# Expert weights as one 8 KB piece per partition, with features, scale, shift and router in that order

## The chip, the cores and the metric

The kernel runs on one core of a Trainium2 chip. Its time is the device time of one execution in microseconds (us), as the median of several runs; lower is better. A core has a matrix engine (PE, with its weight loads listed apart as PEld), a vector engine (DVE), a scalar engine (ACT), GpSimd (POOL), SyncE (SP), which here issues nearly all transfers, and 16 DMA engines that carry them from the chip's main memory (HBM) into the on-chip memory SBUF, which has 128 partitions.

## What is computed

A transformer block with a mixture of experts is followed by a second block of two layers, all in float32, on 256 tokens of 1024 features. The part that the change is about, cut from the reference:

```python
h = modulate(x, norm_ffn_pre, shift, scale)      # rms_norm(x, g) * (1 + scale) + shift
logits = jnp.dot(h, w_router) + b_router
top_logit, top_idx = lax.top_k(logits, TOP_K)    # 4 of 32 experts for each token
gates = jax.nn.softmax(top_logit, axis=-1)
# for each expert e, on the tokens that chose it:
g = h_e @ w_gate[e] + b_gate[e]                  # w_gate, w_up, w_down: 1024 x 1024 each
u = h_e @ w_up[e] + b_up[e]
a = (min(g, 7) * sigmoid(1.702 * min(g, 7))) * (clip(u, -7, 7) + 1)
y_e = a @ w_down[e] + b_down[e]                  # summed over a token's four experts by its gates
```

`shift` and `scale` are two of six modulation vectors, `silu(c) @ w_mod + b_mod`, of 1024 values each. The weights of the 32 experts are 403 MB, all of which are read once.

## The kernel before

**The stream of weights.** Weights pass through a ring of 21 tiles of 128 x 2048 floats (1 MB), in five pools. The class `Stream` has a list of jobs in the order in which the matmuls use them. `pump` (L164) issues the next job's DMA on SP's queue as soon as the job's pool has a free tile; `get` hands the oldest chunk to the matmuls, and `free` gives its tile back. What an engine computes has the order in which the code is written: there is no scheduler. Transfers run as far ahead as free tiles let them.

**The first stage** (`pre_project`, `pre_attend`, `pre_finish`) computes the modulation vectors, the projections, the attention, and the router. Modulation weights come in 24 chunks: eight early ones of 8 x 256 columns per partition, and sixteen late ones, one row of 2048 columns per partition (`add_late`). The late ones are summed on PE (`mod_mm`, L321) or, for the other half, on DVE (`msum`, L314). `mod_fin` then copies the sum to `mrow` (L331), turns it on PE with four transposes into one PSUM bank (L334), and adds the bias `b_mod` on DVE (L338). `mod` then holds a column for each 128 features: column k has features 128 k to 128 k + 127. `gains` (L794 to L796) makes `a2`, (1 + scale) times the gain `norm_ffn_pre`, in the same columns. `pre_finish` turns the tokens' features x into columns (`turned`, L902) and multiplies them with the router's weights `wr` (L913), which are loaded feature 128 k + p into partition p; `router` (L858) multiplies the shift with them.

**The expert stage** (`experts`). Each expert takes twelve chunks of 1 MB: four of `w_gate`, four of `w_up`, four of `w_down`. A chunk is 256 rows of the weight matrix; partition p takes rows p and 128 + p of it (`expert_chunks`), two pieces of 4 KB. An expert works on up to 64 tokens at a time; expert 16 in the order, the one with the most tokens, is run twice on the same chunks, so there are 33 passes. `gather_k` (L1292) gathers the columns of two experts' tokens with one-hot matmuls, where x is the stationary operand (the weight load) and the one-hot matrix `pm` moves, and ACT applies `a2` and the shift on the way out. `up_mm` (L1209) multiplies a chunk of gate or up weights, which moves, with the gathered columns; `turn_h` (L1243) transposes the hidden values, with h as the stationary operand; `down_mm` (L1220) multiplies the down weights; a one-hot matmul (L1362) adds the result into its tokens' rows. Small work (gathers, transposes, scatters) is popped from a list between the chunks. Within a chunk, matmul j takes row pair member j, which must be the feature of column 2 q + j of the gathered tokens: that is what ties the order of rows in a chunk to the order of features everywhere else.

**The last stage** is the second block (`even`, `mlp`, `odd`), whose weights follow the experts' in the same stream.

Of the kernel before, what the change touches and what calls it, by code (L numbers as in the profile page):

```python
# [19 lines left out]
P = 128  # L20
# [97 lines left out]
def one(v, src):  # L118
    return [(v, src)]
# [99 lines left out]
        self.pump()  # L219


class Kernel:
    def __init__(self, tc, I, dbg=None):
        self.tc, self.nc, self.I, self.dbg = tc, tc.nc, I, dbg or {}
# [103 lines left out]
    def mod_fin(self, acc, n):  # L328
        nc = self.nc
        mrow = self.mrow  # L330
        nc.scalar.copy(mrow, acc)  # L331
        b = self.bank()
        for j in range(4):
            nc.tensor.transpose(b[:, j * P : (j + 1) * P], mrow[:, j * P : (j + 1) * P], self.c("ident"))  # L334
        v = b.rearrange("p (j g i) -> p j g i", j=4, g=4)
        o = self.mod[:, 0, 16 * n : 16 * n + 16].rearrange("p (g j) -> p j g", g=4)
        bb = self.V("b_mod")[:, 16 * n : 16 * n + 16].rearrange("p (g j) -> p j g", g=4)
        nc.vector.tensor_tensor(o, v[:, :, :, 0], bb, OP.add)  # L338

    def split_rows(self, hi, lo, v):  # L340

# [23 lines left out]
    def pre_project(self, A, B):  # L365
# [8 lines left out]
        for nm, n in rows:  # L374
            src = I[nm]
            if len(src.shape) == 2:
# [16 lines left out]
        tp = lambda a: a.rearrange("(t p) d -> p t d", p=P)  # L393
        nc.sync.dma_start(out=x, in_=tp(I["x"][0]))
        nc.sync.dma_start(out=xc, in_=tp(I["ctx"][0]))
        also = {("i", 3): [(pc, I["pre"]), (self.wf, I["w_fourier"][0].rearrange("(i g) c d -> (g c) i d", g=2))],
                ("q", 2): [(self.wr, kp(I["w_router"][0])), (self.br, I["b_router"])], ("k", SMALL): self.post_small(),
                ("o", 3): self.expert_bias_in(B)}

        def add(nm, q, cols, f, split=None):  # L400
# [227 lines left out]
    def pre_attend(self, B, C):  # L628
# [95 lines left out]
            self.modulation(MODS[6 + t])  # L724
        st.free(2)
        self.post_turn()
        for i in range(2):
            mix[i] = B.tile([P, 2048], F32R, tag=f"lk{i}", name="mix").rearrange("p (k t) -> p k t", k=KD)
        nc.scalar.activation(C.tile([P, 3], F32, tag="mx", name="mx", bufs=4)[:, 0:1], self.eps[1e-6], AF.Exp)
# [63 lines left out]
        def gains():  # L793
            nc.vector.tensor_tensor(gc, mod[:, 0, 16:24], self.V("norm_attn_post"), OP.mult)  # L794
            nc.vector.tensor_tensor(self.g2, mod[:, 0, 40:48], self.V("norm_ffn_post"), OP.mult)
            nc.vector.scalar_tensor_tensor(self.a2, mod[:, 0, 32:40], 1.0, self.V("norm_ffn_pre"), OP.add, OP.mult)  # L796

        fills = {u: [self.modulation] * FILLS[u] + [gains] * (u == 4) for u in range(5)}
        due = []
# [47 lines left out]
    def pre_finish(self, B, C, R):  # L847
# [50 lines left out]
        def turned(t):  # L898
            for h in range(2):
                b = self.bank()  # L900
                for k in range(4):
                    nc.tensor.transpose(b[:, k * P : (k + 1) * P], x[:, t, (4 * h + k) * P : (4 * h + k + 1) * P], ident)  # L902
                nc.scalar.copy(xT[:, 4 * h : 4 * h + 4, t * P : (t + 1) * P], b.rearrange("p (k t) -> p k t", k=4))

        def norm(t):
# [260 lines left out]
    def expert_chunks(self):  # L1166

        I, st, nc = self.I, self.stream, self.nc
        self.reg = {}

        def src(nm, p, q):
            def f(v):
                w = I[nm][0]
                if p < FIXED:
                    return one(v, w[p, q * 256 : (q + 1) * 256].rearrange("(k p) f -> p k f", p=P))
                if p not in self.reg:
                    self.reg[p] = nc.values_load(self.ids[0:1, p : p + 1], engines=(ENG.SP,), min_val=0, max_val=E - 1)
                return one(v, w[bass.ds(self.reg[p], 1), q * 256 : (q + 1) * 256].rearrange("o (k p) f -> p (o k) f", p=P))
            return f

        for p in range(E + 1):
            if p < E:
                for nm in ("w_gate", "w_up"):
                    for q in range(4):
                        st.add((2, 1024), src(nm, p, q))
            if p:
                for q in range(4):
                    st.add((2, 1024), src("w_down", p - 1, q))
# [50 lines left out]
    def turn_h(self, M, h):  # L1239
        nc = self.nc  # L1240
        b = self.bank("tr", "x")
        for j in range(4):
            nc.tensor.transpose(b[:, j * P : (j + 1) * P], h[:, j * P : (j + 1) * P], self.c("ident"))  # L1243
        ht = M.tile([P, 4, P], F32, tag="ht", name="ht", bufs=2)
        nc.scalar.copy(ht.rearrange("p a b -> p (a b)"), b)
        return ht
# [39 lines left out]
    def gather_k(self, xg, pm, k, n, m):  # L1286

        nc = self.nc
        b = self.bank("xg", "r" if m == 2 else "x")
        for j in range(m):  # L1290
            for t in range(2):
                nc.tensor.matmul(b[:, n * j : n * j + n], self.x[:, t, (k + j) * P : (k + j + 1) * P], pm[:, t, 0:n], start=(t == 0), stop=(t == 1))  # L1292
        for j in range(m):
            nc.scalar.activation(xg[:, k + j], b[:, n * j : n * j + n], AF.Identity,  # L1294
                                 bias=self.mod[:, 0, 24 + k + j : 25 + k + j], scale=self.a2[:, k + j : k + j + 1])
# [163 lines left out]
    def overflow(self, M):  # L1459
# [3 lines left out]
        with tc.If(self.more > 0):  # L1463
# [3 lines left out]
            with tc.For_i(0, self.more, 1) as j:  # L1467
                e = nc.values_load(self.ids[0:1, bass.ds(j + (E + 1), 1)], engines=(ENG.Activation,), min_val=0, max_val=E - 1)

                def weights(nm, q):  # L1470
                    w = self.yw
                    nc.scalar.dma_start(out=w, in_=I[nm][0][bass.ds(e, 1), q * 256 : (q + 1) * 256].rearrange("o (k p) f -> p (o k) f", p=P))
                    return w

                sc = M.tile([E + 1, 2], F32, name="scol")
# [1031 lines left out]
```

## Time and profile before

| | us |
|---|---|
| median of 3 runs | 1805.74 |
| lowest, highest | 1804.57, 1810.54 |
| profiled execution, its own time | 1805.48 |
| its span, from the first to the last instruction | 1803.70 |

| engine | busy us | share of the span |
|---|---|---|
| PE matmuls | 1721.6 | 95% |
| PE weight loads | 1031.0 | 57% |
| DVE | 744.8 | 41% |
| ACT | 583.3 | 32% |
| POOL | 22.8 | 1% |

The core read 550.71 MB from HBM in the span, 306 GB/s in the mean. Shares over the whole span mix three stages with different limits, so they are read stage by stage: the rate of the transfers in each window, and in the chain of waits (followed back from the last instruction) whether a stage's steps are matmuls or transfers. A PE that waits a little for every chunk still counts as busy nearly all the time. [...]

### The profile page before, as it was taken

Reading aid. Unit: us, or ns where it says so; the run is one execution under the profiler, and the core shown is the slowest. Engines: PE = TensorE matmul, PEld = TensorE weight load, DVE = VectorE, ACT = ScalarE, POOL = GpSimd, SP = SyncE. Lnnn points to the kernel's source line nnn. Section 1 sums busy time; section 2 is a strip of 40 time slices with the busy share of each in tenths; the row PEclk is TensorE's granted clock in tenths of the full one; section 3 lists DMA queues with packets and bytes.
Section 4 is the critical chain, followed back from the end, with each engine's and each line's share of the span. In section 5 each row is a group of like instructions: output and inputs, shape, how many; then the busy total and the mean of one; then the engine's idle time right before and its main releaser. Section 6 shows DMA issues by size and latency. Waiting matters only on the chain.

```text
span 1803.7 us, 24461 instructions
## 1 busy us (share of the span) xinstructions
PE 1721.6 (95%) x9553; PEld 1031.0 (57%) x9553; DVE 744.8 (41%) x1604; ACT 583.3 (32%) x1147; POOL 22.8 (1%) x31
## 2 busy tenths in 40 slices
PE   8989999999999999999998998899999999999998
PEld 6756543333333333333332332588699989989997
DVE  4675522222221112212211112576665558756554
ACT  5534311111111111111111110555654446545444
POOL 0000000000000000000000000100000001000000
PEclk9999999999999999999999999999999999999999
DMA  9987899999999999999999999986165563345540
GB/s 351 327 278 278 322 386 410 411 412 412 412 412 411 411 412 412 413 412 411 411 412 413 413 413 412 312 241 189 48 210 187 187 186 129 131 139 196 185 147 24
DMA packets 202461, 553.45 MB, mean 307 GB/s; under 512 B 11136, under 2 KB 87430, under 8 KB 200294
## 3 DMA queue, kind: packets, MB, share of 16 engines
q1 hardware_dynamic: 201290, 550.35, 80.9%
q8 instruction: 76, 1.25, 0.3%
q0 software_dynamic: 576, 0.86, 0.2%
q10 hardware_dynamic: 476, 0.64, 0.1%
q14 instruction: 43, 0.35, 0.1%
HBM read 550.71 MB, written 1.07 MB: 306 GB/s over the span
## 4 chain that ended last, share of the span: by engine, by line
PE 72%; DMA 18%; DVE 6%; ACT 3%; issue 1%; SPq 0%; ACTq 0%; DVEq 0%
PE acc L1795 11%; PE g L1209 10%; PE u L1209 10%; PE ot L1780 10%; PE y L1220 8%; DMA ring<-in_w_gate 7%; DMA ring<-in_w_up 5%; DMA ring<-in_w_down 4%; PE pj L1780 4%; PE xg L1292 3%; PE pj L1787 2%; PE yb L1362 1%; PE bk L542 1%; PE mix L363 1%; DVE msum L314 1%
## 5 line engine op out<-in xcount | busy, mean ns | idle before, releaser
L1566 DVE TENSOR_TENSOR ring<-ring,ring 128x1024 fp32r<-128x1024 f32 (+1 forms) x200 | 234.3, 1215 | 77.8 <-ACT ring L1565 77.3
L1209 PE MATMUL g<-ring,xg 128*64 128x512 f32 x1056 | 254.9, 605 | 8.8 <-DMA ring<-in_w_gate 8.7
L1209 PE MATMUL u<-ring,xg 128*64 128x512 f32 x1056 | 248.2, 602 | 10.0 <-DMA ring<-in_w_up 9.2
L1220 PE MATMUL y<-ring,ht 128*64 128x512 f32 x1056 | 240.8, 598 | 16.2 <-DMA ring<-in_w_down 15.7
L1565 ACT CAST ring<-ring 128x1024 fp32r<-128x1024 f32 (+1 forms) x200 | 198.5, 1046 | 75.7 <-PE acc L1795 54.3
L1281 ACT ACTIVATE z<-y,gsl 64x512 fp32r<-64x512 f32 x66 | 45.0, 682 | 429.1 <-PE y L1220 402.1
L1780 PE MATMUL ot<-ahi,ring 128*128 128x256 f32 x960 | 177.2, 282 | 0.0
L1220 PEld LDWEIGHTS y<-ring,ht 128*64 128x64 f32 x1056 | 70.0, 136 | 164.7 <-issue 117.0
L1282 DVE SCALAR_TENSOR_TENSOR z<-y,gsl,z 64x512 fp32r<-64x512 f32 x66 | 49.5, 750 | 251.0 <-ACT z L1281 250.9
L1780 PEld LDWEIGHTS ot<-ahi,ring 128*128 128x128 f32 x960 | 151.3, 191 | 1.3
L1209 PEld LDWEIGHTS u<-ring,xg 128*64 128x64 f32 x1056 | 67.3, 136 | 131.9 <-issue 99.3
L1209 PEld LDWEIGHTS g<-ring,xg 128*64 128x64 f32 x1056 | 67.2, 137 | 128.6 <-issue 118.9
L1780 PE MATMUL ot<-alo,ring 128*128 128x256 f32 x480 | 135.6, 283 | 0.0
L1795 PE MATMUL acc<-ring,hhi 128*128 128x512 f32 x480 | 131.5, 395 | 0.0
L1795 PEld LDWEIGHTS acc<-ring,hhi 128*128 128x128 f32 x480 | 88.1, 188 | 19.0
L1228 ACT ACTIVATE sg<-gm 128x512 f32<-128x512 f32 x33 | 20.8, 630 | 239.5 <-DVE gm L1227 239.5
L1780 PEld LDWEIGHTS ot<-alo,ring 128*128 128x128 f32 x480 | 91.8, 191 | 1.3
L1294 ACT ACTIVATE xg<-xg,mod,a 128x128 f32<-128x128 f32 (+1 forms) x136 | 50.9, 452 | 99.2 <-PE xg L1292 99.2
L1292 PEld LDWEIGHTS xg<-pm,x 128*128 128x128 f32 x544 | 65.2, 195 | 26.8 <-issue 15.4
L1780 PE MATMUL pj<-ahi,ring 128*128 128x256 f32 x416 | 79.9, 287 | 0.0
L1271 DVE TENSOR_SCALAR gt<-gt,cp 128x256 fp32r<-128x256 f32 x33 | 16.0, 484 | 150.6 <-PE gt L1269 150.6
L1795 PE MATMUL acc<-ring,hlo 128*128 128x512 f32 x240 | 75.4, 395 | 0.0
(518 smaller groups left out, 2080.5 us busy)
## 6 DMA issues: line engine op xcount, KB each, us to landing
ring<-in_w_gate SPq DMA_DIRECT2D x128, 1024.0 KB, 17.9
ring<-in_w_up SPq DMA_DIRECT2D x128, 1024.0 KB, 17.9
ring<-in_w_down SPq DMA_DIRECT2D x128, 1024.0 KB, 17.9
ring<-in_mlp_w SPq DMA_DIRECT2D x64, 1024.0 KB, 5.4
ring<-in_w_mod SPq DMA_DIRECT2D x24, 1024.0 KB, 6.4
ring<-in_odd_w_in SPq DMA_DIRECT2D x12, 1024.0 KB, 5.3
ring<-in_even_w_in SPq DMA_DIRECT2D x7, 1024.0 KB
ring<-in_w_out SPq DMA_DIRECT2D x4, 1024.0 KB, 5.0
```

The source lines that it names most:

```text
L1209: nc.tensor.matmul(acc[64 * h : 64 * h + 64], xg[:, 2 * q + j], w[:, j, 512 * h : 512 * h + 512], start=(q == 0 and j == 0), stop=False, s ...
L1220: nc.tensor.matmul(acc[64 * h : 64 * h + 64], l, w[:, j, 512 * h : 512 * h + 512], start=(q == 0 and j == 0), stop=(q == 3 and j == 1), sk ...
L1228: nc.scalar.activation(sg, gm, AF.Sigmoid, scale=1.702)
L1281: nc.scalar.mul(t[s], a[s], g[s])
L1282: nc.vector.scalar_tensor_tensor(t[o], a[s], g[s], t[s].bitcast(F32), OP.mult, OP.subtract)
L1292: nc.tensor.matmul(b[:, n * j : n * j + n], self.x[:, t, (k + j) * P : (k + j + 1) * P], pm[:, t, 0:n], start=(t == 0), stop=(t == 1))
L1294: nc.scalar.activation(xg[:, k + j], b[:, n * j : n * j + n], AF.Identity, bias=self.mod[:, 0, 24 + k + j : 25 + k + j], scale=self.a2[:, ...
L1565: nc.scalar.copy(hi[:, c], v[:, c])
L1566: nc.vector.tensor_tensor(lo[:, c], v[:, c], hi[:, c].bitcast(F32), OP.subtract)
L1780: nc.tensor.matmul(out, w[a][:, k, c : c + n], x[b][:, k], start=(k == 0 and i == 0), stop=(k == KD - 1 and i == 2))
L1787: nc.tensor.matmul(out, x[a][:, k, t * P : (t + 1) * P], w[b][:, k, c : c + n], start=(k == 0 and i == 0), stop=(k == KD - 1 and i == 2))
L1795: nc.tensor.matmul(acc[2 * t + n], x[a][kx][:, t * P : (t + 1) * P], w[b][:, j, 512 * n : 512 * n + 512], start=(first and i == 0), stop=( ...
```

## The change

An expert chunk stays 256 rows, but partition p now takes rows 2 p and 2 p + 1, which are neighbours in memory: one piece of 8 KB in place of two of 4 KB. Column 2 q + j of the features is then every second feature of block q, beginning at j, and everything that meets the expert weights takes that order: the gathers and the turned x (with a step of two floats in the stationary operand), the hidden values ahead of the down matmuls, the router's weights, and the shift, scale and gain. The modulation vectors of the attention keep the old order, so `mod_fin` makes half of its 16 columns in each order, and the reordered biases and gain are loaded apart (`vp`, two DMAs) and turned into columns (`vcp`).

```diff
+def pairs(k):
+    return slice(256 * (k // 2) + k % 2, 256 * (k // 2) + 256, 2)
...
         nc.scalar.copy(mrow, acc)
-        b = self.bank()
-        for j in range(4):
-            nc.tensor.transpose(b[:, j * P : (j + 1) * P], mrow[:, j * P : (j + 1) * P], self.c("ident"))
-        v = b.rearrange("p (j g i) -> p j g i", j=4, g=4)
-        o = self.mod[:, 0, 16 * n : 16 * n + 16].rearrange("p (g j) -> p j g", g=4)
-        bb = self.V("b_mod")[:, 16 * n : 16 * n + 16].rearrange("p (g j) -> p j g", g=4)
-        nc.vector.tensor_tensor(o, v[:, :, :, 0], bb, OP.add)
+        for kind in range(2):
+            b = self.bank()
+            for j in range(4):
+                s = pairs(j) if kind else slice(j * P, (j + 1) * P)
+                nc.tensor.transpose(b[:, j * P : (j + 1) * P], mrow[:, s], self.c("ident"))
+            g = slice(0, 2) if kind == n - 1 else slice(2, 4)
+            v = b.rearrange("p (j g i) -> p j g i", j=4, g=4)[:, :, g, 0]
+            c = 16 * n + 4 * g.start
+            o = self.mod[:, 0, c : c + 8].rearrange("p (g j) -> p j g", g=2)
+            bb = self.vcp[:, c - 16 : c - 8] if kind else self.V("b_mod")[:, c : c + 8]
+            nc.vector.tensor_tensor(o, v, bb.rearrange("p (g j) -> p j g", g=2), OP.add)
...
+        self.vp = B.tile([12, 256], F32, name="vp")
+        vp = [(self.vp[0:4], I["norm_ffn_pre"][0].rearrange("(q f) -> q f", f=256)),
+              (self.vp[4:12], I["b_mod"][0][24 * P : 40 * P].rearrange("(q f) -> q f", f=256))]
...
-                ("q", 2): [(self.wr, kp(I["w_router"][0])), (self.br, I["b_router"])], ("k", SMALL): self.post_small(),
+                ("q", 2): [(self.wr.rearrange("p (q j) e -> p q (j e)", j=2), I["w_router"][0].rearrange("(q p j) e -> p q (j e)", p=P, j=2)),
+                           (self.br, I["b_router"])] + vp, ("k", SMALL): self.post_small(),
...
         self.post_turn()
+        vcp = self.vcp = B.tile([P, 24], F32, name="vcp")
+        b = self.bank()
+        for j in range(2):
+            nc.tensor.transpose(b[:, 12 * j : 12 * j + 12], self.vp[:, j:256:2], self.c("ident", 12)[:, 0:12])
+        nc.vector.tensor_copy(vcp.rearrange("p (r j) -> p j r", j=2), b[:, 0:24].rearrange("p (j r) -> p j r", j=2))
...
-            nc.vector.scalar_tensor_tensor(self.a2, mod[:, 0, 32:40], 1.0, self.V("norm_ffn_pre"), OP.add, OP.mult)
+            nc.vector.scalar_tensor_tensor(self.a2, mod[:, 0, 32:40], 1.0, self.vcp[:, 0:8], OP.add, OP.mult)
...
-                    nc.tensor.transpose(b[:, k * P : (k + 1) * P], x[:, t, (4 * h + k) * P : (4 * h + k + 1) * P], ident)
+                    nc.tensor.transpose(b[:, k * P : (k + 1) * P], x[:, t, pairs(4 * h + k)], ident)
...
+                v = v.rearrange("p k f -> p (k f)")
                 if p < FIXED:
-                    return one(v, w[p, q * 256 : (q + 1) * 256].rearrange("(k p) f -> p k f", p=P))
+                    return one(v, w[p, q * 256 : (q + 1) * 256].rearrange("(p k) f -> p (k f)", p=P))
...
-                return one(v, w[bass.ds(self.reg[p], 1), q * 256 : (q + 1) * 256].rearrange("o (k p) f -> p (o k) f", p=P))
+                return one(v, w[bass.ds(self.reg[p], 1), q * 256 : (q + 1) * 256].rearrange("o (p k) f -> p (o k f)", p=P))
...
-            nc.tensor.transpose(b[:, j * P : (j + 1) * P], h[:, j * P : (j + 1) * P], self.c("ident"))
+            nc.tensor.transpose(b[:, j * P : (j + 1) * P], h[:, pairs(j)], self.c("ident"))
...
-                nc.tensor.matmul(b[:, n * j : n * j + n], self.x[:, t, (k + j) * P : (k + j + 1) * P], pm[:, t, 0:n], start=(t == 0), stop=(t == 1))
+                nc.tensor.matmul(b[:, n * j : n * j + n], self.x[:, t, pairs(k + j)], pm[:, t, 0:n], start=(t == 0), stop=(t == 1))
```

The same is done for the expert loads of `overflow`, a loop for experts whose tokens don't fit.

The order of instructions changes in the first stage alone. On PE, during the attention, before: the first of the two calls of `mod_fin` (line 334, four transposes of `mrow`), between a chunk's modulation matmuls and the scores (`sc`) of the next pair of heads.

```order
L752 MATMUL sc<-krl_1042,qs 128x512
L321 MATMUL macc<-ring_1022,csil 32x512 x4
L334 MATMUL bk<-cp,mrow 128x128 x4
L745 MATMUL sc<-kn,qn 128x512 x2
L776 MATMUL tr<-cp,prob 128x128 x8
```

The same place on PE now:

```order
L772 MATMUL sc<-krl_1045,qs 128x512
L327 MATMUL macc<-ring_1025,csil 32x512 x4
L343 MATMUL bk<-cp,mrow 128x128 x8
L765 MATMUL sc<-kn,qn 128x512 x2
L796 MATMUL tr<-cp,prob 128x128 x8
```

Eight transposes stand there in place of four; nothing else changed its place. On SP's queue, before, the loads around the router's weights `wr` and bias `br`, between chunks of modulation weights and of `w_kv_up`:

```order
L164 DMA ring_519<-in_w_q_up 128x3x384
L164 DMA wr<-in_w_router 128x8x32
L164 DMA br<-in_b_router 1x32
L164 DMA ring_531<-in_w_mod 128x2048
L164 DMA ring_566<-in_w_kv_up 128x2x768
```

The same place on SP's queue now:

```order
L164 DMA ring_520<-in_w_q_up 128x3x384
L164 DMA wr<-in_w_router 128x4x64
L164 DMA br<-in_b_router 1x32
L164 DMA vp<-in_norm_ffn_pre 4x256
L164 DMA vp<-in_b_mod 8x256
L164 DMA ring_534<-in_w_mod 128x2048
L164 DMA ring_569<-in_w_kv_up 128x2x768
```

The two loads of `vp` moved in ahead of a chunk of modulation weights, and the router's pieces are 64 floats long in place of 32.

## Rows read from the trace of the kernel before

**Rows 1.** The page's slices (45 us each): the rate of the transfers.

```profile
GB/s 351 327 278 278 322 386 410 411 412 412 412 412 411 411 412 412 413 412 411 411 412 413 413 413 412 312 241 189 48 210 187 187 186 129 131 139 196 185 147 24
```

**Rows 2.** Windows: us, busy by engine (instructions), PE clock, DMA share, GB/s.

```profile
205.00:248.00 43.00, 42.24 (x219) 18.36 (x217) 13.37 (x53) 8.54 (x19) 0.00 (x0) 0.99 0.94 343
248.00:1144.00 896.00, 859.27 (x3932) 312.62 (x3928) 183.94 (x381) 129.22 (x251) 0.00 (x0) 1.00 1.02 411
900.00:914.00 14.00, 11.51 (x48) 3.14 (x48) 2.77 (x4) 0.63 (x1) 0.00 (x0) 1.00 1.02 418
915.00:954.00 39.00, 36.09 (x173) 13.94 (x171) 8.00 (x18) 6.95 (x14) 0.00 (x0) 1.00 1.03 410
85.00:89.00 4.00, 4.00 (x22) 2.36 (x21) 3.39 (x9) 1.52 (x4) 0.00 (x0) 1.00 1.03 422
92.00:106.00 14.00, 12.75 (x72) 9.97 (x65) 11.35 (x21) 5.00 (x12) 0.00 (x0) 1.00 0.97 359
...
1144.00:1803.70 659.70, 636.48 (x4338) 561.79 (x4338) 418.31 (x859) 348.88 (x676) 14.96 (x14) 1.00 0.51 162
```

**Rows 3.** The chain of waits, expert stage: start us, us, what.

```profile
203.58 2.81 PE g L1209 x8
...
412.07 7.02 PE y L1220 x32
...
465.50 7.02 PE y L1220 x32
...
1126.09 17.90 DMA ring<-in_w_down
1144.02 9.41 DMA ring<-in_even_w_in
```

**Rows 4.** Timeline of PE: start, us, instruction, idle before and its releaser.

```profile
972.36 1.94 PE L1220 MATMUL y<-ring,ht 128*64 128x512 f32 x8 [0.86 <-DMA ring<-in_w_down]
974.93 1.94 PE L1220 MATMUL y<-ring,ht 128*64 128x512 f32 x8 [0.63 <-DMA ring<-in_w_down]
```

**Rows 5.** DMA view, 85 to 89 us: packets by size; queue: packets, MB, share.

```profile
DMA packets 229, 1.69 MB, mean 422 GB/s; under 512 B 23, under 2 KB 23, under 8 KB 23
...
q1 hardware_dynamic: 229, 1.69, 103.3%
```

**Rows 6.** DMA view, 248 to 1144 us.

```profile
DMA packets 96389, 368.20 MB, mean 411 GB/s; under 512 B 5612, under 2 KB 6947, under 8 KB 96340
...
q1 hardware_dynamic: 96340, 367.54, 102.2%
```

**Rows 7.** DMA view, 21 to 26 us.

```profile
DMA packets 1171, 1.87 MB, mean 375 GB/s; under 512 B 24, under 2 KB 923, under 8 KB 1171
...
q1 hardware_dynamic: 1171, 1.87, 106.6%
```

**Rows 8.** Groups of weight loads: name, shapes, count, busy us, mean ns, idle before.

```profile
L1292 PEld LDWEIGHTS xg<-pm,x 128*128 128x128 f32 x544 | 65.2, 195 | 26.8 <-issue 15.4 <-ACT xg L1294 10.5 <-DVE ngm L1026 0.7
...
L1243 PEld LDWEIGHTS tr<-cp,gm 128*128 128x128 f32 x132 | 13.8, 140 | 27.2 <-issue 17.8 <-DVE z L1282 7.3 <-PE g L1209 1.3
```

**Rows 9.** The chain of waits, first stage.

```profile
116.22 0.13 DVE vc L1678
...
126.15 0.66 PE bk L334 x4
...
138.45 0.66 PE bk L334 x4
```

**Rows 10.** Two tiles: small loads on SP's queue (ns); waits for the modulation weights.

```profile
L164 SPq DMA_DIRECT2D vr<-in_mix_norm x1: 465/465/465, 57.9 to 57.9; - x1
L164 SPq DMA_DIRECT2D vr<-in_mlp_norm x1: 411/411/411, 58.4 to 58.4; - x1
...
  PEld macc L481: 1.0, 1
  PE macc L481: 0.8, 1
```

More of the change, by code (lines that the diff above doesn't have):

```diff
@@ L1471, in weights @@
                     w = self.yw
-                    nc.scalar.dma_start(out=w, in_=I[nm][0][bass.ds(e, 1), q * 256 : (q + 1) * 256].rearrange("o (k p) f -> p (o k) f", p=P))
+                    nc.scalar.dma_start(out=w.rearrange("p k f -> p (k f)"), in_=I[nm][0][bass.ds(e, 1), q * 256 : (q + 1) * 256].rearrange("o (p k) f -> p (o k f)", p=P))
                     return w
```

## The prediction

> **What bounds the kernel now.** I read the page's slices first. Their rate line shows three stages: a restless first stage, a long flat one at 410 to 413 GB/s, and a last one at half that and less [rows 1]. The windows give the flat stage its edges: from 248 to 1144 us the core moves data at 411 GB/s and the DMA engines are busy for more than the whole time (a share of 1.02, since the records of successive pieces overlap a little), while from 205 to 248 us it is 343 GB/s [rows 2]. That flat stage is the mixture of experts, 896 of the 1803.7 us.
>
> Does the PE array or the transfer end that stage? The chain of waits answers it differently in the stage's two halves [rows 3]. Around 440 us it runs through PE: the y matmuls of one expert start at 412.07, those of the expert two later at 465.50 us. So PE needs 53.43 us for two experts, 26.7 us each, when data lies ready. At that pace it eats 24 chunks of 1.05 MB in 53.43 us, 471 GB/s, faster than the transfers bring them; the chunks that were loaded ahead run out, and at the end of the stage the chain is transfers: 17.90 us from the issue of the last w_down chunk to 1144 us, then 9.41 us for the first chunk of the next block. The timeline of PE near 975 us shows how that looks: 1.94 us of matmuls per chunk, then 0.6 to 0.9 us of waiting for the next landing, again and again [rows 4].
>
> How much could PE give back if transfers were free? 33 passes (32 experts, one of them twice) at 26.7 us from the first gate matmul at 203.58 us [rows 3] end at 1085 us. The transfers end at 1144. So some 59 us can be won by faster transfers before PE becomes the bound, and all of it would reach the end: the 659.7 us after 1144 wait for the landings that close the stage.
>
> **The change part by part.**
>
> *The pieces.* Each of the 384 expert chunks is now 128 pieces of 8 KB in place of 256 of 4 KB. The bytes stay. What counts is the rate that 8 KB pieces reach on a busy queue, and the kernel before already has such pieces: the sixteen late chunks of modulation weights are one 8 KB row per partition. In the 4 us from 85 to 89 us nothing else of weight moves (229 pieces, 23 of them under 512 B, so 206 of 8 KB [rows 5]), the engines are as busy as in the flat stage (1.03), and the rate is 422 GB/s [rows 2]. The flat stage moves 368.20 MB [rows 6]; at 422 GB/s that is 872.5 us, 23.5 less than 896.
>
> Bounds. Below: the 4 KB pieces alone run at 418 GB/s in some stretches and at 410 in others [rows 2], so 422 may be a good stretch, and the gain may be nothing, or a loss (rivals). Above: the time per piece. In the flat stage 102.2% of 16 engines' 896 us went to 96340 pieces, 6947 of them small [rows 6]; that is 163.9 ns for one of 4 KB, 327.8 for two, if the small ones cost nothing. In the window from 21 to 26 us most pieces are of 1 KB (923 less 24 small ones) and 248 are of 3.75 KB [rows 7]: 106.6% of 16 x 5000 ns over 1147 pieces and 1.87 MB. A straight line through both windows, with a fixed part and a part per KB, has a fixed part of some 15 ns and some 37 ns per KB. One fixed part saved per 8 KB is 15 of 328 ns, 4.6%, 41 us. The estimate of 15 ns comes from a mixed window, and the 8 KB pieces themselves took 321 ns (103.3% of 16 x 4000 ns over 206 [rows 5]), 2.1% less than 328. I take the measured 8 KB rate: **23.5 us less**, with 0 and 41 as ends. The engines' queue gets half as many pieces per chunk; loads may be issued further ahead for it, which I cost at nothing, since a full queue doesn't go faster for being longer.
>
> *The strided reads.* A weight load of PE now takes every second column of x (the gathers) or of h (the transposes ahead of the down matmul). Their number and size stay. The trace has no load with such a step. They are 544 loads, 65.2 us, and 132 loads, 13.8 us [rows 8]. Bounds: nothing, and double, 79 us of PE over 33 passes, 2.4 us per pass. I take nothing, because of the next room: with the transfers 23.5 us shorter, PE still has 59 - 23.5 = 35 us of slack, 1.07 us per pass, so up to a load time 1.45 times as long the cost hides behind the transfers. Its other end is a rival. The 16 transposes ahead of the router change the same way; doubled, they'd add some 2 us, inside the range.
>
> *The modulation columns.* Twice, at 126 and 138 us, four transposes turn a modulation row into columns, 0.66 us each time, and both stand on the chain [rows 9]. Now eight stand there, and the add on DVE is cut in two. PE goes on to the scores behind them, so 0.66 us more each time, 1.3 us. The second add (on DVE, off the chain) and one more bank of six per call cost nothing that I can see.
>
> *The reordered constants.* Two small transposes and one copy on DVE make the reordered scale and shift. A like copy, of 64 columns, is on the chain for 0.13 us [rows 9]: 0.1 us. Two more DMAs on SP's queue, of the kind that takes 0.465 and 0.411 us to issue [rows 10], hold up what SP issues next, the next chunk of modulation weights, by 0.9 us. In the whole trace nobody waits for those chunks but two matmuls of an earlier line, together under 2 us [rows 10]; without that cover it would be 0.9 us. The router's weights come in pieces of 256 B, half as many as before; that is under 1 us of transfer in a stage that has gaps.
>
> The sum, against the profiled execution, whose time is 1805.48 us around a span of 1803.70: 1805.5 - 23.5 + 1.3 + 0.1 = **1783.4 us**. The median of the runs is 1805.74, the same within 0.3 us. About 0.3% either way, 5 us, is what a measurement can tell from no change.
>
> **The rivals.**
>
> *The rate doesn't rise.* If 411 GB/s is a limit of bytes and not of pieces, only the small costs are left: 1806.9. For it: the flat line hardly moves in 900 us [rows 1]. Against it: 4 KB pieces themselves reach 418, and 8 KB ones 422 [rows 2]. 8%.
>
> *Half a gain.* The 85 to 89 us window may have caught a favourable stretch, as 900 to 914 us is one of the 4 KB pieces. Scaled by their mean over their best, 411/418, 422 becomes 415 GB/s: 368.2 MB in 887 us, 9 us less, 1798. 8%. [...]
>
> *Strided weight loads are slow (slower than before).* Doubled, the loads add 79 us to PE's 1085 us, with the 1.4 us ahead 1166, 22 us past 1144: 1827. PE then is the bound and the transfers don't matter. It decides from 1.07 us per pass on. For it: no row shows a stepped load. Against it: only the time is unknown, not the amount of data. 6%. [...]
>
> *Long pieces stall (slower).* From 92 to 106 us 8 KB pieces ran at 359 GB/s with a share of 0.97 [rows 2], 370 for a full queue. The flat stage would take 995 us, 99 more: 1906. Against it: the 4 KB expert pieces do no better right after starts (343 GB/s from 205 to 248 us), and once the queue stays full it passes; those rows also lie 24 KB apart, the expert pieces follow one another. 4%.
>
> **How the numbers follow.** The forecast has 74%, its own range 1768 to 1796 (a gain of 9 to 39 us after the small costs). With half a gain 82% are faster by over 0.3%, 8% within 0.3%, 10% slower. The range takes in the upper bound of the gain, 41 us, 1766, and below it reaches to half a gain and stops at 1803: what is left out is the slower rivals and most of the unchanged rate, under 2 in 10.
>
> **What would show it.** In the profile after: some 49,000 pieces fewer, the flat stage at 420 to 425 GB/s, the last w_down landing near 1122 us, the loads of the gather still near 120 ns of busy time each (65.2 us over 544), the chain's end of that stage still transfers, eight transposes of 1.3 us at about 127 and 139 us, and nothing changed behind the stage but its start. Wrong would be: a rate of 411 (pieces don't matter); PE without waits at the end of the stage (the strided loads cost); a rate of 422 but a time that fell by much less (the gain was given back behind 1122 us, at the loads of the next block).

## The result, and the profile after

The changed kernel takes 1785.72 us in the median of four runs (1784.11 to 1787.47); the kernel before, on the same chip, 1808.14 us (1804.57 to 1812.72). The ratio is 0.9875, its 95% interval 0.9847 to 0.9902. A second set on another chip gave 1782.84 against 1807.67 us, 0.9859 (0.9834 to 0.9885). (Of the four runs before, three are those whose median, 1805.74 us, stands ahead; the fourth took 1812.72.) So the kernel is 22 to 25 us faster by the medians; the forecast was 1783.4 us, 22 below its profiled execution.

The profiled execution of the changed kernel is the slowest of its four, 1787.47 us, with a span of 1785.7 us. Line numbers move: the gate and up matmuls L1209 are L1230, the down matmul L1220 is L1241, the gather L1292 is L1313, the transposes ahead of the down matmul L1243 are L1264, those of `mod_fin` L334 are L343.

The rate line of the page, to be laid beside [rows 1], in slices of 44.6 us:

```profile
GB/s 350 293 304 243 347 385 421 422 422 422 422 423 420 421 422 422 423 422 422 422 422 422 422 423 421 293 224 158 74 193 185 187 189 143 128 144 190 188 142 24
```

The flat stage stands at 420 to 423 where it stood at 410 to 413. Its windows, with the columns of [rows 2]:

```profile
205.00:248.00 43.00, 42.24 (x225) 19.60 (x226) 15.51 (x72) 10.49 (x27) 0.00 (x0) 1.00 0.96 372
...
248.00:1125.00 877.00, 860.30 (x3941) 322.41 (x3937) 184.74 (x382) 129.55 (x251) 0.00 (x0) 1.00 1.01 421
900.00:914.00 14.00, 13.67 (x61) 4.91 (x63) 3.17 (x5) 1.96 (x3) 0.00 (x0) 1.00 1.01 422
915.00:954.00 39.00, 37.31 (x177) 14.66 (x177) 8.42 (x19) 6.23 (x13) 0.00 (x0) 1.00 1.01 422
```

The engines are as full as before (a share of 1.01 for 1.02), and the same bytes go through in less time. The transfer view of that stretch, as [rows 6]:

```profile
DMA packets 51907, 369.05 MB, mean 421 GB/s; under 512 B 5619, under 2 KB 7072, under 8 KB 7072
...
q1 hardware_dynamic: 51858, 368.40, 100.9%
```

44,482 fewer pieces in the stage for the same 368 MB; over the whole span the queue counts 151,650 pieces, 49,640 fewer than the 201,290 before. No piece between 2 KB and 8 KB is left here.

The chain of waits through the expert stage, as [rows 3] (start us, us, what):

```profile
415.54 7.02 PE y L1241 x32
...
469.36 7.02 PE y L1241 x32
...
1105.86 19.72 DMA ring<-in_w_down
1125.58 9.31 DMA ring<-in_even_w_in
```

In its first half the chain still runs through PE, 53.82 us for two experts (53.43 before). At its end it is still transfers. The stage ends at 1125.58 us for 1144.02: 18.4 us earlier, and the span is 18.0 us shorter. What follows takes 660.1 us (659.7 before), so the whole gain is made in this stage, and none is given back behind it. Nor is it all of the gain: this execution lost some 2 us in its first stage, in front of any changed instruction (the modulation chunk ahead of the router's weights is already issued at 48.75 us for 46.69), and its first gate matmul starts at 206.37 us (203.50 before). From there to the end of the last down matmul it is 921.2 us for 942.5, 21.3 less.

PE at the end of the stage, as [rows 4] (start, us, instruction, idle before and its releaser):

```profile
960.45 1.94 PE L1241 MATMUL y<-ring,ht 128*64 128x512 f32 x8 [0.55 <-DMA ring<-in_w_down]
...
1125.62 1.94 PE L1241 MATMUL y<-ring,ht 128*64 128x512 f32 x8 [0.59 <-DMA ring<-in_w_down]
```

The waits shown are shorter, 0.55 and 0.59 us in place of 0.6 to 0.9, but they are there up to the last down matmul: the transfers remain the bound.

The weight loads with a step of two floats, as [rows 8]:

```profile
L1313 PEld LDWEIGHTS xg<-pm,x 128*128 128x128 f32 x544 | 67.1, 196 | 26.4 <-issue 15.4 <-ACT xg L1315 10.5 <-DVE ngm L1046 0.3
...
L1264 PEld LDWEIGHTS tr<-cp,gm 128*128 128x128 f32 x132 | 18.3, 208 | 27.2 <-issue 14.6 <-DVE z L1303 11.4 <-PE g L1230 1.3
```

The gather's loads hardly change, 67.1 us for 65.2 and 196 ns for 195. Those of the transposes take 208 ns in place of 140, half as much again; the 16 transposes ahead of the router do the same, 209 ns for 140.

The first stage's chain, as [rows 9]:

```profile
119.76 0.14 DVE vc L1699
119.89 0.09 DVE vcp L746
...
128.81 1.13 PE bk L343 x8
...
142.01 1.13 PE bk L343 x8
```

The eight transposes take 1.13 us where four took 0.66, and the copy that the reordered constants need takes 0.09.

### The profile page after: what moved, and what is told of

The parts are those of the page before. It is cut to its first block, busy times and chain, and to the rows that moved or that the text cites. A ratio compares the mean times of both kernels' runs of the same rounds, so it can differ in the third digit from the quotient of the medians.

```text
span 1785.7 us, 24489 instructions
## 1 busy us (share of the span) xinstructions
PE 1723.7 (97%) x9563; PEld 1044.1 (58%) x9563; DVE 745.2 (42%) x1607; ACT 584.7 (33%) x1147; POOL 22.8 (1%) x31
## 3 DMA queue, kind: packets, MB, share of 16 engines
q1 hardware_dynamic: 151650, 550.36, 79.6%
HBM read 550.72 MB, written 1.07 MB: 309 GB/s over the span
## 4 chain that ended last, share of the span: by engine, by line
PE 77%; DMA 13%; DVE 5%; ACT 3%; issue 1%; SPq 0%; ACTq 0%; DVEq 0%
PE g L1230 12%; PE acc L1816 11%; PE u L1230 10%; PE ot L1801 10%; PE y L1241 9%; DMA ring<-in_w_gate 6%; PE pj L1801 4%; DMA ring<-in_w_up 3%; PE xg L1313 3%; DMA ring<-in_w_down 2%; PE yb L1383 2%; PE bk L557 2%; PE pj L1808 2%; PE tr L1264 1%; DVE msum L320 1%
## 5 line engine op out<-in xcount | busy, mean ns | idle before, releaser
L1230 PE MATMUL g<-ring,xg 128*64 128x512 f32 x1056 | 253.7, 602 | 3.9 <-DMA ring<-in_w_gate 3.9
L1230 PE MATMUL u<-ring,xg 128*64 128x512 f32 x1056 | 246.9, 601 | 4.9 <-DMA ring<-in_w_up 4.9
L1241 PE MATMUL y<-ring,ht 128*64 128x512 f32 x1056 | 237.4, 597 | 6.6 <-DMA ring<-in_w_down 6.2
L1241 PEld LDWEIGHTS y<-ring,ht 128*64 128x64 f32 x1056 | 71.4, 136 | 149.9 <-issue 126.5
L1230 PEld LDWEIGHTS u<-ring,xg 128*64 128x64 f32 x1056 | 67.8, 136 | 124.2 <-issue 103.8
L1230 PEld LDWEIGHTS g<-ring,xg 128*64 128x64 f32 x1056 | 66.8, 136 | 120.1 <-issue 110.2
L1313 PEld LDWEIGHTS xg<-pm,x 128*128 128x128 f32 x544 | 67.1, 196 | 26.4 <-issue 15.4
L1292 DVE TENSOR_SCALAR gt<-gt,cp 128x256 fp32r<-128x256 f32 x33 | 16.0, 484 | 147.4 <-PE gt L1290 147.4
```

Source lines behind the costliest of these rows:

```text
L1230: nc.tensor.matmul(acc[64 * h : 64 * h + 64], xg[:, 2 * q + j], w[:, j, 512 * h : 512 * h + 512], start=(q == 0 and j == 0), stop=False, s ...
L1241: nc.tensor.matmul(acc[64 * h : 64 * h + 64], l, w[:, j, 512 * h : 512 * h + 512], start=(q == 0 and j == 0), stop=(q == 3 and j == 1), sk ...
L1313: nc.tensor.matmul(b[:, n * j : n * j + n], self.x[:, t, pairs(k + j)], pm[:, t, 0:n], start=(t == 0), stop=(t == 1))
```

## The experiments

The theory: a piece carries a fixed price on a full queue, the change halves the number of pieces, and PE has room for what the new order costs it. The rivals: that it is the order of the rows in memory and not the length of the pieces; that PE is about to become the bound; and, once the rates were seen, that the place of the ring's tiles on the chip takes part. All rates below are of one stretch, 300 to 1080 us, in which every kernel moves expert chunks alone. There the kernel before shows

```profile
DMA packets 83211, 321.20 MB, mean 412 GB/s; under 512 B 4892, under 2 KB 4892, under 8 KB 83170
...
q1 hardware_dynamic: 83170, 320.65, 102.3%
```

and the changed one

```profile
DMA packets 45140, 329.02 MB, mean 422 GB/s; under 512 B 5007, under 2 KB 5007, under 8 KB 5007
```

Three sets were measured, each with its own runs of the kernel before on the same chip: the first has its median at 1807.67 us, the second at 1808.03, the third at 1809.35.

### First set: length or order

**The change again**, as the measure for the set:

> The changed kernel as it is, beside the others of this set. All theories: about 0.9875 of the kernel before, some 22 us less; the flat stage at 422 GB/s.

Measured: 1782.84 us, the ratio given above. Its last down chunk lands at 1122.14 us, where the prediction had put it.

**The new order in 4 KB pieces.** Rows 2p and 2p+1 are fetched by two DMAs, so that the order of the change stays and its long pieces go:

```diff
-                v = v.rearrange("p k f -> p (k f)")
+                two = lambda s: [(v[:, k], s[:, k]) for k in range(2)]
...
-                    return one(v, w[p, q * 256 : (q + 1) * 256].rearrange("(p k) f -> p (k f)", p=P))
+                    return two(w[p, q * 256 : (q + 1) * 256].rearrange("(p k) f -> p k f", p=P))
```

> The changed kernel, but each expert chunk is loaded by two DMAs, the first with rows 2p, the second with rows 2p+1: the pieces are of 4 KB again, while the order of features, the strided reads, the doubled transposes and the neighbouring rows stay. Theory (a fixed cost per piece, saved by longer pieces): the flat stage is back at 411 GB/s and the time is that of the kernel before plus the small costs of the new order, 1.4 to 4 us, ratio 1.000 to 1.003. Rival (what helps is that a partition reads neighbouring rows of memory, not the length of a piece): still about 422 GB/s, ratio near 0.99.

Measured: 1811.34 us, ratio 1.0014 (1.0002 to 1.0025). The transfer view:

```profile
DMA packets 87681, 319.73 MB, mean 410 GB/s; under 512 B 9735, under 2 KB 9735, under 8 KB 87632
```

**The old order by two DMAs**, which tells what two DMAs per chunk cost by themselves. The same edit in the kernel before, rows p and 128 + p:

```diff
+                two = lambda s: [(v[:, k], s[:, k]) for k in range(2)]
...
-                    return one(v, w[p, q * 256 : (q + 1) * 256].rearrange("(k p) f -> p k f", p=P))
+                    return two(w[p, q * 256 : (q + 1) * 256].rearrange("(k p) f -> p k f", p=P))
```

> Control for the run with two DMAs: the kernel before, with each expert chunk loaded by two DMAs of 4 KB pieces (rows p, then rows 128 + p). Theory: the number of DMAs doesn't matter, since SP has 2.5 us per chunk and an issue takes about 0.4 us; 411 GB/s, ratio 0.998 to 1.003. Rival (a DMA has a cost of its own on the busy queue): slower by 384 such costs, with 0.05 us each 19 us, ratio 1.01.

Measured: 1814.1 us, ratio 1.0023 (1.0008 to 1.0039), and the same rate:

```profile
DMA packets 87612, 319.47 MB, mean 410 GB/s; under 512 B 9729, under 2 KB 9729, under 8 KB 87563
```

Two DMAs cost some 0.2%. Beside that control the new order in 4 KB pieces is no slower and no faster (their intervals overlap), although each of its DMAs skips every second row: which rows a partition takes shows no worth in this pair, to the gain or against it. All that the strided loads, the eight transposes and the two more loads on SP's queue cost together is below what this pair can tell.

**8 KB pieces alone.** The kernel before, with the pieces of the change and nothing else of it. It leaves out the order of the features that goes with them, so its result is not the block's; the work is the same in number and size:

```diff
+                v = v.rearrange("p k f -> p (k f)")
...
-                    return one(v, w[p, q * 256 : (q + 1) * 256].rearrange("(k p) f -> p k f", p=P))
+                    return one(v, w[p, q * 256 : (q + 1) * 256].rearrange("(p k) f -> p (k f)", p=P))
```

> The kernel before with the 8 KB pieces alone: the expert chunks take neighbouring rows, everything else stays in the old order, so the expert matmuls pair rows and features that don't belong together; the work is the same in number and size. It gives the gross gain of the pieces, without the costs of the new order. Theory: 422 GB/s and 1.4 to 5 us less than the changed kernel, 23.5 to 27 us less than the kernel before, ratio 0.985 to 0.987. Rival (the strided reads or the doubled transposes cost as much as the pieces gain in places): ratio below 0.983.

Measured: 1786.75 us, ratio 0.9879 (0.9852 to 0.9906).

```profile
DMA packets 45146, 329.04 MB, mean 422 GB/s; under 512 B 5010, under 2 KB 5010, under 8 KB 5010
```

The whole rate of the change, 422 GB/s, and the whole gain come with this one edit. It was expected 1.4 to 5 us faster than the full change, as a gain without the small costs would be, and came out 3.9 slower, which the intervals don't tell apart. From the first gate matmul to the last down matmul it takes 921.0 us, the change 921.2 and, in the run above, 920.4: what the new order costs in this stage is no more than the 0.8 us between two executions of one kernel.

### Second set: the price of a piece, and the room on PE

**2 KB pieces.** The kernel before, two DMAs for the two halves of the columns:

```diff
+                two = lambda s: [(v[:, :, c : c + 512], s[:, :, c : c + 512]) for c in (0, 512)]
...
-                    return one(v, w[p, q * 256 : (q + 1) * 256].rearrange("(k p) f -> p k f", p=P))
+                    return two(w[p, q * 256 : (q + 1) * 256].rearrange("(k p) f -> p k f", p=P))
```

> The kernel before with each expert chunk loaded by two DMAs that take one half of the columns each: pieces of 2 KB, four per partition and chunk. From the two rates, 8 KB take 8192 x 16 / 422 = 310.6 ns as one piece and 318.9 ns as two, so a piece has a fixed cost of some 8.3 ns. Theory (that cost per piece): four pieces take 335.5 ns, 391 GB/s; 368 MB then take 942 us in place of 896, 46 us more, ratio near 1.025. Rival (the cost is only 3.5 ns per piece, and the rest of the gain comes from elsewhere): 326 ns, 402 GB/s, 20 us more, ratio 1.011. Second rival (4 KB pieces are already at a limit of bytes): ratio 1.00.

Measured: 1861.7 us, ratio 1.0299 (1.0268 to 1.0331), 53.7 us more.

```profile
DMA packets 157409, 303.94 MB, mean 390 GB/s; under 512 B 9255, under 2 KB 9255, under 8 KB 157363
...
q1 hardware_dynamic: 157363, 303.36, 104.6%
```

That is what a price per piece does. Sixteen engines at 390, 412 and 422 GB/s take 84.0, 159.1 and 310.6 ns for a piece of 2, 4 and 8 KB. Twice the shorter less the longer is 8.9 ns in the one step and 7.6 in the other: about the same amount each time, some 8 ns, at these three lengths. The 3.5 ns of the rival was the author's estimate, an amount that no run shows. (Of two DMAs in place of one, the control says 2 GB/s and 0.2%, which is part of the difference between 8.9 and 7.6 and between the 54 us measured and the 46 expected.)

**The transposes twice.** In the changed kernel each transpose ahead of the down matmul is made a second time:

```diff
-        for j in range(4):
+        for j in (0, 1, 2, 3, 0, 1, 2, 3):
```

> The changed kernel with the four transposes of the hidden values done twice in each of the 33 passes: about 0.7 us more of PE per pass, 23 us in all. It measures the slack that hid the strided reads. With 26.9 us per pass when data lies ready, PE alone would end the stage near 1094 us, 31 us before the transfers, 0.95 us per pass. Theory (transfers still set the end): within 3 us of the changed kernel. Rival (PE is the bound, or nearly): some 20 us more than the changed kernel.

Measured: 1783.42 us, ratio 0.9874 (0.9843 to 0.9905): no change against the 0.9859 of the change. The window of the stage shows where it went (columns of [rows 2]), first for the change again:

```profile
248.00:1122.00 874.00, 857.41 (x3930) 321.65 (x3926) 183.63 (x381) 129.38 (x251) 0.00 (x0) 1.00 1.01 421
```

and with the transposes twice:

```profile
248.00:1122.00 874.00, 868.28 (x4057) 338.29 (x4054) 183.27 (x380) 129.38 (x251) 0.00 (x0) 1.00 1.01 421
```

PE works 10.9 us more (the expectation had 23), out of 16.6 us of idle time, and the rate stays at 421. So the slower loads of these transposes, some 9 us of them at the most (132 by 68 ns), are hidden too.

**The gathers twice**, twice as much strided work again:

```diff
-        for j in range(m):
+        for j in list(range(m)) * 2:
```

> The changed kernel with each gather's matmuls done twice: 4.2 us more of PE for two passes, 2.1 us per pass, 69 us in all, which is about what the strided weight loads would have cost had they doubled. Theory (the slack is about 1 us per pass): PE becomes the bound, its 1094 us become some 1163, 37 us past the landings, so 30 to 45 us more than the changed kernel; the chain of the stage is matmuls. Rival (the slack is much larger, and only transfers count): within 5 us of the changed kernel.

Measured: 1834.94 us, ratio 1.0151 (1.0125 to 1.0177): 52 us above the change, more than either theory had said. The window:

```profile
248.00:1122.00 874.00, 873.25 (x4265) 368.72 (x4264) 176.15 (x367) 122.03 (x240) 0.00 (x0) 1.00 1.00 412
```

PE has 0.75 us of idle time left in 874, and the transfers wait for it. The timeline gives the two lengths that matter, that of two experts and that of the stage, and what follows it:

```profile
416.11 0.74 PE L1264 MATMUL tr<-cp,gm 128*128 128x128 f32 x4
...
473.70 0.74 PE L1264 MATMUL tr<-cp,gm 128*128 128x128 f32 x4
...
1162.77 5.37 PE L1241 MATMUL y<-ring,ht 128*64 128x512 f32 x24
...
1177.40 5.10 POOL L1603 TENSOR_TENSOR ring<-ring,ring 128x1024 fp32r<-128x1024 f32 x2 [975.65 <-DMA ring<-scr]
1177.50 6.87 DVE L1577 SCALAR_TENSOR_TENSOR x<-ring,r,x 128x512 f32<-128x512 f32 x4 [2.76 <-PEq L1484]
...
1186.21 2.15 PE L1794 MATMUL pj<-ahi,ring 128*128 128x256 f32 x16
```

Two experts take 57.59 us in place of 53.82, 1.89 us more per pass, 62 us in 33 passes. The last down matmul ends at 1168.14 us in place of 1127.56, 40.6 us later. So 62 - 40.6, some 21 us, fitted into PE's waits, and no more. The expectation took the 35 us of slack of the prediction; that is where it missed. Another 5.7 us were lost behind the stage (663.8 us from its last matmul to the end, for 658.1). There the first matmul of the next block comes 18.1 us after the last down matmul, in place of 10.5. In the changed kernel the four instructions by which DVE adds the experts' sum to x (L1577) are nearly done when GpSimd begins its two subtractions (L1603):

```profile
1134.56 2.74 DVE L1577 SCALAR_TENSOR_TENSOR x<-ring,r,x 128x512 f32<-128x512 f32 x4 [0.26 <-DVEq L1484]
...
1136.98 4.94 POOL L1603 TENSOR_TENSOR ring<-ring,ring 128x1024 fp32r<-128x1024 f32 x2 [932.78 <-ACT ring L1600]
```

With the gathers made twice they begin 9.4 us after the last down matmul in place of 7.0, together with GpSimd's. The two additions that run beside a subtraction take 2.80 and 2.83 us, the other two 0.74; in the changed kernel all four take 0.75. The late start and the slow additions make 6.5 of the 7.5 us. The rest of the 52 us lies between these two profiled runs, 46.3 us apart, and the medians.

### Where the tiles lie

The prediction had left one thing unexplained: stretches of 418 GB/s beside others of 410 in the kernel before [rows 2]. The trace's records of single pieces show a pattern. Taken in the order of the chunks, the 4 KB pieces of most chunks take some 164 ns in the mean and those of the others 159; the 8 KB pieces of the changed kernel take 313 to 315 and 309 to 310, and it comes round every 21 chunks. 21 is the number of tiles in the ring. They are held by five pools. The 13 tiles of the first two, A and B, begin 192 bytes behind a multiple of 256 bytes of their partition; the five of C and D, which are laid out from the other end of the partition, 224 bytes; the three of E begin on a multiple. So the place may matter. But it is not simply each tile's own place: as far as the order tells the chunks apart, some five of the 21 are fast, those into E and the two into A that follow them.

**Rings A and B moved by 64 bytes**, to a multiple of 256. In the changed kernel a tile that nobody uses is put in front of them:

```diff
+        K.pad = per.tile([P, 16], F32, name="pad")
```

> The changed kernel with 64 bytes more in front of the first two of the five pools of ring tiles, so that their tiles, 13 of 21, begin at a multiple of 256 bytes (they began 192 bytes past one); the third and fourth pool, 5 tiles, stay 224 bytes past one, the last, 3 tiles, was on one already. In both traces the pieces have two durations that change with a period of 21 chunks, 309 and 314 ns for 8 KB, 159 and 164 ns for 4 KB. Theory (a piece whose place begins off a multiple of 256 bytes takes some 4 to 5 ns more): the shorter duration now holds in about 16 of 21 chunks, the flat stage goes from 422 to some 426 GB/s and the time falls by 6 to 9 us against the changed kernel. Rival (the two durations come from something else): the same time as the changed kernel within 2 us.

Measured: 1773.51 us (1773.36 to 1777.07), ratio 0.9807 (0.9783 to 0.9832).

```profile
DMA packets 45642, 332.62 MB, mean 426 GB/s; under 512 B 5069, under 2 KB 5069, under 8 KB 5069
...
q1 hardware_dynamic: 45599, 332.04, 100.9%
```

Nearly all pieces (98.8%) now take 309 ns and the rate is 425 to 427 GB/s in every slice of the flat stage. The expectation had 6 to 9 us, and some 16 of 21 chunks fast; the five into C and D, which weren't moved, are fast too. Against the 1783.42 us of the same set (the change with work that was shown to be hidden), that is another 10 us. This version beats both kernels.

### Third set: is it the place?

**The kernel before, moved by 64 bytes**, the same line in it:

> The kernel before, with 4 KB pieces, and 64 bytes more in front of the first two pools of ring tiles, as in the run on the changed kernel that this brought to 426 GB/s. Theory (a place off a multiple of 256 bytes costs some 4 to 5 ns per piece, whatever its length): 159 ns for nearly all 4 KB pieces, the flat stage at 418 GB/s in place of 411, 368 MB in 881 us, 15 us less than the kernel before, ratio 0.991 to 0.993. Rival (the gain there belongs to 8 KB pieces alone): ratio 0.998 to 1.002.

Measured: 1792.28 us, ratio 0.9901 (0.9875 to 0.9927).

```profile
DMA packets 84784, 327.27 MB, mean 420 GB/s; under 512 B 4986, under 2 KB 4986, under 8 KB 84742
...
q1 hardware_dynamic: 84742, 326.70, 102.3%
```

The place acts alone, at 4 KB pieces too: 420 GB/s for 412, and nearly all pieces (95%) at 159 ns.

**The same 64 bytes behind the rings**, so that A and B stay and the working tiles after them move (a pool of its own, opened behind ring B):

```diff
+        K.pad = es.enter_context(tc.tile_pool(name="pad", bufs=1)).tile([P, 16], F32, name="pad")
```

> The changed kernel with the 64 bytes behind the first two pools of ring tiles: those stay where they were, 192 bytes past a multiple of 256, and only what lies behind them (the working tiles of each stage) moves by 64 bytes. Theory (the place of the ring tiles counts): as the changed kernel, 422 GB/s, ratio near 0.987. Rival (the place of the working tiles, which the engines read while chunks land, made the difference): 426 GB/s and some 10 us less than the changed kernel, ratio near 0.981.

Measured: 1783.51 us, ratio 0.9854 (0.9824 to 0.9883); the rate is that of the change:

```profile
DMA packets 45145, 329.03 MB, mean 422 GB/s; under 512 B 5011, under 2 KB 5011, under 8 KB 5011
```

**Moved by 128 and by 32 bytes**: A and B at 64 and at 224 bytes behind a multiple of 256 (32 floats, 8 floats in the tile of the first edit).

> The changed kernel with 128 bytes in front of the first two pools: their tiles begin 64 bytes past a multiple of 256. Theory (only a multiple of 256 is free of the extra 4 to 5 ns): 314 ns in some 16 of 21 chunks again, 422 GB/s, ratio near 0.987. Rival (any place but 192 past is free of it): 309 ns, 426 GB/s, ratio near 0.981.

> The changed kernel with 32 bytes in front of the first two pools: their tiles begin 224 bytes past a multiple of 256, as those of the third and fourth pool always do. In the run moved by 64 bytes all pieces took 309 ns, those into the third and fourth pool too. Theory (a multiple of 256 is wanted): 314 ns again, near 422 GB/s, ratio near 0.987. Rival (224 past is free as well, as the third and fourth pool suggest): 426 GB/s, ratio near 0.981.

Measured: 1784.4 us, ratio 0.9858 (0.9833 to 0.9883), and 1788.71 us, ratio 0.9888 (0.986 to 0.9915). The first one's transfer view:

```profile
DMA packets 45152, 329.09 MB, mean 422 GB/s; under 512 B 5010, under 2 KB 5010, under 8 KB 5010
```

and the second one's:

```profile
DMA packets 45048, 328.31 MB, mean 421 GB/s; under 512 B 5002, under 2 KB 5002, under 8 KB 5002
```

Of four places of A and B, one is fast (0) and three are slow (64, 192, 224). It is the place of A and B and not that of the working tiles, and it isn't that anything has moved at all.

## Why the prediction was right

**The pieces.** The term of 23.5 us carries the result, and its mechanism held: half as many pieces on a queue that stays full. Chunks in the old order with 8 KB pieces have the rate and the gain (422 GB/s, 1786.75 us); the new order with 4 KB pieces has neither (410 GB/s, 1811.34 us). That a longer queue brings no rate of its own shows in the kernel before: 412 GB/s from 260 to 300 us, where a `w_gate` chunk takes 10.0 us from issue to landing, and 413 from 1000 to 1080 us, where it takes 17.6. The medians put the gain at 22.4 and 24.8 us, the profiled pair at 18.0, with a late first stage in it, and the stage by itself at 21.3. The time lies in both ranges that the prediction names, 1768 to 1796 and, with half a gain in it, 1766 to 1803. The upper bound of 41 us, from a fixed part of 15 ns, was too high by about two: some 8 ns show between 2, 4 and 8 KB.

That the 8 KB modulation rows had the rate of the expert stage to a digit, 422 GB/s [rows 2, 5], is in part luck. In the trace of the kernel before, the 6 us from 84 to 90 us have 382 GB/s and the 2 us from 85 to 87 us 426. Of the 206 pieces of the window that was taken, 198 took 309 ns and seven 436 to 941 ns, which makes a mean of 320. From 300 to 1080 us after the change 44 of 40,105 take over 330 ns, but 70% take 311 to 321. Two different mixtures came to one rate; where nearly all take 309 ns, in the rings moved by 64 bytes, it is 426.

**The rivals on the rate.** "The rate doesn't rise" is refuted by the rate line (420 to 423 GB/s for 410 to 413). "Half a gain" feared that the window was a favourable stretch, like those of 418 GB/s. By its 309 ns it was one, and its seven long pieces hid that; but the good stretches belong to the pattern of the tiles, and don't scale the rate of 8 KB pieces the way I scaled it. With A and B in the slow place, 4 and 8 KB pieces differ by 2.4% (412 and 422 GB/s). With A and B on the multiple they differ by 1.6% (327.27 and 332.62 MB in the same 780 us), some 5 ns per piece. So part of what a piece cost here goes with the place of the tiles.

**The strided reads.** The amount was taken as nothing, from no row. For the gather that is right, 196 ns for 195. For the transposes nothing was too little: with the same step of two they take 208 ns for 140. Together they make 0.2 us per pass (53.82 - 53.43 us for two experts), 6 us of PE in 33 passes, and they are hidden, as the prediction had argued from the slack.

**The slack.** Here a number was wrong that the time didn't show. The prediction had 59 us before and 35 after the change. The gathers made twice show 21 us after it, and with the 18.4 us by which the stage moved, 40 before. PE's idle time in the windows of the stage says nearly the same: 896.00 - 859.27 = 36.7 us before, which stood in [rows 2], and 877.00 - 860.30 = 16.7 after. The working left out that the stage holds more than 33 equal passes: with the gathers made twice, 33 passes of 28.8 us from the first gate matmul at 205.66 us would end at 1156 us, and the last down matmul ends at 1168. The rival of slow strided loads would thus have decided from 0.65 us per pass, not 1.07. The real cost of 0.2 us was well below either, so the verdict on it stands. But the upper bound of the gain, 41 us, would have used up all the slack, where the prediction saw 18 to spare.

**The small costs.** The eight transposes were put at 0.66 us more each time; they cost 0.47 (1.13 for eight less 0.66 for four), 0.9 us in all for 1.3. The copy took 0.09 us for 0.1. The two more loads on SP's queue left no mark. All of it together is a microsecond, and no run could resolve it.

**Long pieces that stall.** No slice of the flat stage in any kernel with 8 KB pieces falls back towards 359 GB/s, with one exception that has another cause: with the gathers made twice PE is the bound, and one slice falls to 321 while the transfers wait for it. What happened at 92 to 106 us [rows 2] belongs to that stage.

So the time was right for the reason given; that it came so near is in part luck. What the prediction had not seen is that the place of the tiles is part of a piece's price; moving A and B gives 10 us more with the change and 17 without it.

## What to carry to other kernels

Where a stage stands at a flat rate with a DMA share of about 1, count its pieces: at 4 KB each some 2% of the time went with their number here (412 and 422 GB/s), at 2 KB some 8% against 8 KB (390 and 422 GB/s), and an order of rows that makes a partition's share one run in memory gave the 2% back, with all readers of the other operand following. A stretch elsewhere in the same trace that already has the new piece size told the rate better than a fit did here; look at its neighbours and its single pieces too before trusting the digit. Before a cost is called hidden, read the covering engine's idle time in the stage's window, and load that engine on purpose: here the slack on PE was 17 to 21 us where the passes had promised 35.

## What was not expected of the hardware

- **The place of 13 ring tiles takes part in the time of most pieces of the stage.** With A and B at 192 bytes behind a multiple of 256 bytes of the partition, as in the change, the 8 KB pieces of some 16 of 21 chunks took 313 to 315 ns in the mean; with them on the multiple, nearly all took 309 (426 GB/s for 422). For 4 KB pieces it is 164 and 159 ns: the same 4 to 5 ns at either length. At 64 and at 224 bytes the rate is nearly that of 192, 422 and 421 GB/s for 422, so the size doesn't follow the distance. Nor is it each tile's own place: the five tiles of C and D stay at 224 bytes in every run, and their pieces are slow in the changed kernel, with A and B off the multiple, and fast, 309 ns, when they are on it; and the modulation rows from 85 to 89 us [rows 5], all into tiles of A at 192 bytes, took 309 ns but for a few. Which of A and B matters, and whether moving C and D would change anything, was not tried, nor was any place of A and B but these four, so 256 bytes is not shown to be the step that counts. The cause is open, and only the effect of the place of A and B is shown.
- **A transposing weight load with a step of two floats takes 208 ns for 140**, while the gather's load, which is not a transpose, takes 196 ns with the step and 195 without.
- **An addition on DVE took 2.8 us in place of 0.74 while GpSimd subtracted beside it.** It came to light where PE was made the bound: DVE's work then began later and met GpSimd's, and the next block's first matmul waited for both delays.
